# Weight blocks that are not written back, stores on a second queue, and regrouped visits, in a two-layer hybrid encoder

## The chip, the cores and the metric

The kernel runs on one core of a Trainium2 chip. Its time is the device time in microseconds of one execution; lower is better.

## The reference

Two layers of a mixer are applied to a prompt of 1024 rows and to 8 × 16 sample rows, with a model width of 1024. In each layer a projection `w_in` feeds three mixers whose outputs are gated, concatenated, projected by `w_out` and added to the input under a layer norm:

```python
h = x @ w_in
uA, vA, zA, qB, fB, iB, zB, qC, kC, vC, zC = jnp.split(h, split_pts, axis=-1)
yA, vA_rows = sgu(uA, vA, ln_v_g, ln_v_b, w_s, b_s)            # A: spatial gating
oB, S_new = hgrn2_scan(qh, kh, vh, logf)                       # B: linear recurrence
oC = swa_prompt(q, k, v, sinks)                                # C: windowed attention
mix = jnp.concatenate([yA, yB, yC], axis=-1)
out = layer_norm(DEEPNORM_ALPHA * x + mix @ w_out, ln_g, ln_b)
```

The recurrence B keeps a 64 × 64 state for each of 4 heads and goes chunk by chunk. The attention C has 8 query heads and 2 key heads, chunks of 64 and a window of 128, so that a tile of 128 rows sees at most two bands of keys, its own tile and the one before.

## The kernel before

Rows are cut into tiles of 128; eight tiles of the prompt and one of samples (`"s"`) form three groups of three tiles (`GROUPS`, L45). The kernel goes through the groups of layer 0, then those of layer 1, six in all. Within a group the columns of the projection are cut into blocks of 256. The order of blocks and side work in a group is a string (L47): for the first one `K Q0 Q1 -BX +C +X I F Q +B ZB U Z -C C0 C1 +N -X V +A`. A name is a weight block, + starts a piece of side work, - finishes it. K, Q0, Q1 are columns of the attention (blocks 9, 7, 8 of `w_in`), I and F those of the recurrence (5 and 4); after them come blocks 3, 6, 0, 2, 10, 11, 1 of `w_in`. Later groups also run the four `w_out` blocks O0 to O3 of the group before.

A product is made in three passes from high and low parts of both operands, so each weight block (1024 × 256 numbers, 1 MB) is split on chip. `issue_w` (L270 to L315) takes the next block of the list `wlist`. Where the block is met for the first time, it is loaded raw from DRAM in four pieces of 256 KB (L297) into the staging ring `wst` (four buffers; the first three blocks borrow others); `piece` (L299 to L312) then makes the high part `wh` with a copy on ACT (L125) and the low part `wl` with a subtraction on DVE or POOL (L142), and after each second piece stores 512 KB of either part to DRAM (L306, L307), on SP's queue. Where a layer's later groups meet the block again, both parts are loaded back (L288, L289), 2 MB. `wh` and `wl` have two buffers each.

A block's matmuls are written in `prod` (L349 to L359): 24 matmuls of 128 rows of depth each, eight with the high parts of both sides and two times eight with one low part. `tok_major` makes a result of 128 × 256 for a tile, `feat_major` one of 128 × 384 for 128 columns and all tiles. After each such result `tick` runs one visit of every open lane of side work, and the lanes' small matmuls come between the 24 of one result and the 24 of the next. PE's order is thus written by hand; other engines and queues are ordered by the framework under priorities.

Lane C is the attention (`lane_c`, L501 on). Its work goes block by block (tile and key head) through stages that lie some visits apart: scores with masks (L459, L466), softmax on DVE and ACT (L470 to L480), transposes of the probabilities (`p_transpose`, L488, copied by ACT to one of three `pT` buffers), and `attend` (L497), the product with the values. A block has two visits for each stage; of its two bands one is treated in each:

```python
                if ph == 0:
                    pso[u] = AXT([P, 2, P])
                if ph < len(bs):
                    attend(g, pso[u], bs[ph][1], pps.pop((u, ph)), ph == 0, ph == len(bs) - 1,
```

Lane B is the recurrence (`lane_b`, L669 on), a few visits for each tile. In a tile's first visit PE transposes keys (L682, copied by ACT to `kvt`), makes decay sums (L688, copied by ACT to `w4s`, a `t1b` buffer), and the chunk-local scores `psA` (L701 to L716), which DVE masks. Then `fin` runs for the tile before (L732): it transposes that tile's output, a `t1b` buffer that DVE has finished (L842), and splits the result into `mixh` and `mixl`. Then the transposes of `w4s` follow (L736). The next visit makes the new state's sums (`psk`, L771), the next the output (L826).

The sample tile and lanes A and X (spatial gating; transposes of x and output rows) are as they are in both kernels.

Of the kernel before, what the change touches and what calls it, by code (L numbers as in the profile page):

```python
# [8 lines left out]
F32 = mybir.dt.float32  # L9
# [11 lines left out]
P = 128  # L21
# [8 lines left out]
NC4 = 3  # L30
PPT = 1
NEA = 3
WDVE0 = (0, 1, 2, 3)
ACT_NORM = (3, 2, 4, 4, 1, 0)
POOL_OPS = ('mgzfy', 'mDrVyf', 'mgDrzVXQfw', 'mgzf', 'mgDrVyf', 'mgrVQfw')
# [61 lines left out]
def body(ctx: ExitStack, tc: tile.TileContext, A, O, cst):  # L97
# [22 lines left out]
    def AXT(shape):  # L120
        uid[0] += 1
        return ps_ax.tile(shape, F32, tag="ax", name=f"ax_{uid[0]}")
# [152 lines left out]
    def issue_w(off=WP):  # L275
        if wpos[0] >= len(wlist):
            return
        l, name, blk = wlist[wpos[0]]
        early = wpos[0] if wpos[0] < NEA else None
        eng_lo = WDVE0 if early is not None else WDVE[l]  # L280
        wpos[0] += 1
        key = (l, name, blk)
        with tc.high_priority(offset=off):
            wh, wl = T("wh", [P, 8, CB], 2, F32R), T("wl", [P, 8, CB], 2, F32R)
            if key in kept:
                for h in range(2):
                    ks = slice(4 * h, 4 * h + 4)
                    nc.sync.dma_start(wh[:, ks, :].bitcast(F32), kept[key][0][:, ks, :])  # L288
                    nc.sync.dma_start(wl[:, ks, :].bitcast(F32), kept[key][1][:, ks, :])  # L289
                wq.append((wh, wl))  # L290
                return
            nm = f"{name}{l}_{blk}"
            kept[key] = [dp.tile([P, 8, CB], F32, tag=nm + c, name=nm + c) for c in "hl"]
            for kk in range(4):
                tag, bufs = ("wst", NWST) if early is None or kk == 3 else ("pT", 3) if early % 2 == 0 else ("c4", NC4)
                st = T(tag, [P, 2, CB], bufs)
                ld = nc.sync.dma_start(st, A[name][l, :, blk, 2 * kk:2 * kk + 2, :])  # L297

                def piece(kk=kk, st=st, tag=tag, bufs=bufs, ld=ld):  # L299
                    hw, lw = wh[:, 2 * kk:2 * kk + 2, :], wl[:, 2 * kk:2 * kk + 2, :]  # L300
                    with tc.high_priority(offset=WP):
                        copy(hw, st)
                        up = tt(dve if kk in eng_lo else pool, lw, st, hw.bitcast(F32), ALU.subtract)
                        if kk % 2:
                            ks = slice(2 * kk - 2, 2 * kk + 2)
                            nc.sync.dma_start(kept[key][0][:, ks, :], wh[:, ks, :].bitcast(F32))  # L306
                            nc.sync.dma_start(kept[key][1][:, ks, :], wl[:, ks, :].bitcast(F32))  # L307
                    acquire(tag, bufs, ld)
                    release(tag, up)
                pieces.append(piece)  # L310
        wq.append((wh, wl))
# [190 lines left out]
    def lane_c(l, tiles, qks, vvs, vprev, oT, vd):  # L502
        todo = [(tl, t) for tl, t in enumerate(tiles) if t != "s"]
        nt = len(todo)
        smp = nt < 3
        blocks = []
        for n, (tl, t) in enumerate(todo):
            for g in range(2):
                bs = [(1 - t % 2, vvs[tl - 1] if tl else vprev)] if t else []
                blocks.append((n, tl, t, g, bs + [(t % 2, vvs[tl])]))  # L510
        qT = transposes(qks[0], todo[0][1] % 2)
        yield
        pts, pps, pso = {}, {}, {}
        nb = len(blocks)
        for k in range(2 * nb + LATT):
            u, ph = divmod(k - LATT, 2)
            if 0 <= u < nb:
                n, tl, t, g, bs = blocks[u]
                if ph == 0:
                    pso[u] = AXT([P, 2, P])  # L520
                if ph < len(bs):
                    attend(g, pso[u], bs[ph][1], pps.pop((u, ph)), ph == 0, ph == len(bs) - 1,
                           oT[:, :, tl * P:(tl + 1) * P])
            u, ph = divmod(k - LPT, 2)
            if 0 <= u < nb:
                bs = blocks[u][4]
                if ph < len(bs):
                    pps[(u, ph)] = p_transpose(pts[u], bs[ph][0], ph == len(bs) - 1)
            u, ph = divmod(k, 2)
            if ph == 0 and u < nb:  # L530
                n, tl, t, g, bs = blocks[u]
                pts[u] = scores(l, t, g, qT)
                if g == 1 and n + 1 < nt:
                    qT = transposes(qks[todo[n + 1][0]], todo[n + 1][1] % 2)
            yield
        if smp:
            yield from attn_sample(l, qks[2], vd, oT[:, :, 2 * P:3 * P])
# [131 lines left out]
    def lane_b(l, tiles, q2, kk, G, zb, vts):  # L669
# [5 lines left out]
        for tl, t in enumerate(tiles):  # L675
# [50 lines left out]
            for u in range(2):  # L726
                au = AT.rearrange("p (c u) t -> p u c t", u=2)[:, u]
                tt(dve, au, psA[u][:, :, 0:64], mA.unsqueeze(1).to_broadcast([P, 2, 64]), ALU.mult)
                for w in range(2):
                    ws = slice(32 * w, 32 * w + 32)  # L730
                    dve.copy_predicated(au[:, :, ws], m4[:, ws].unsqueeze(1).to_broadcast([P, 2, 32]), psA[u][:, :, 64:96])
            if fin is not None:  # L732
                fin()
            psw = AXT([P, 2, P])
            for i in range(2):
                pe.transpose(psw[:, i, :], w4s[:, i, :], idn)  # L736
# [26 lines left out]
                put_state(0)  # L763
            yield

            if not smp:
                psk = [AXT([P, 2, 64]) for _ in range(2)]
                for c in range(2):
# [393 lines left out]
```

## Time and profile before

| | |
|---|---|
| time, median of three runs | 1124.96 us (1124.52 to 1125.7) |
| the profiled execution's own time | 1125.85 us |
| its span | 1124.1 us |
| PE busy | 1080.9 us (96%) |
| DVE, ACT, POOL busy | 652.5, 503.8, 367.8 us |
| mean granted TensorE clock | 0.979 |
| DMA: one hardware queue | 272.66 MB, 69.1% of 16 engines' span |

The span is what lies between the first and the last instruction of the profiled execution; its own time is 1.75 us more. In a row of a timeline the first number is the start in us, the second how long a run of like instructions lasted; the brackets tell how long the engine was idle before and what ended that. Matmuls follow one another in the pipeline, so a row's end overlaps the next row's start; distances between starts tell what a group costs. "PEclk" is the clock that TensorE was granted, as a share of the full one.

### The profile page before, as it was taken

The numbers are of one execution on the slowest core, as the hardware profiler recorded it, in microseconds if no ns is written. First come the engines' busy times: TensorE is split into PE (matmuls) and PEld (weight loads), VectorE is DVE, ScalarE is ACT, GpSimd is POOL, SyncE is SP. The second block draws the span as 40 slices with busy tenths as digits, with TensorE's granted clock in tenths as the row PEclk, the third lists the DMA queues.
The fourth block names the chain that finished last, engine by engine and source line by source line (L and its number), as shares of the span: only waits on it lengthen the run. The fifth ranks groups of instructions, "written<-read, shape, count | busy, mean of one in ns | idle before, by whom it ended". The sixth has DMA issues, their size and how long they took to land. (4 is left out here: it accounts for less than half of the span.)

```text
span 1124.1 us, 25834 instructions
## 1 busy us (share of the span) xinstructions
PE 1080.9 (96%) x10267; PEld 1003.2 (89%) x10267; DVE 652.5 (58%) x1704; ACT 503.8 (45%) x1277; POOL 367.8 (33%) x490
## 2 busy tenths in 40 slices
PE   8598899999999999999999998999999999999996
PEld 7597789989899998998999897999989999889996
DVE  3359753765285355366459668457545636736744
ACT  5286743554433276334256754346443323443310
POOL 3135434432044102384304456141315121214502
PEclk9698999999999999999999999999999999999998
DMA  9994568867557647656966998776856685476463
GB/s 327 362 328 161 197 232 300 298 240 278 199 201 269 235 164 260 234 207 228 343 225 221 324 330 289 244 269 247 275 183 233 208 274 187 173 280 226 155 224 131
DMA packets 88521, 274.31 MB, mean 244 GB/s; under 512 B 10448, under 2 KB 14032, under 8 KB 88400
## 3 DMA queue, kind: packets, MB, share of 16 engines
q1 hardware_dynamic: 88400, 272.66, 69.1%
q8 instruction: 81, 1.33, 0.5%
q14 instruction: 40, 0.33, 0.1%
HBM read 193.97 MB, written 78.64 MB: 243 GB/s over the span
## 5 line engine op out<-in xcount | busy, mean ns | idle before, releaser
L142 POOL TENSOR_TENSOR wl<-wst,wh 128x512 fp32r<-128x512 f32 x58 | 84.6, 1472 | 210.2 <-ACT wh L125 126.2
L359 PE MATMUL mm<-wh,xh 128*128 128x256 f32 x864 | 129.7, 292 | 16.2 <-ACT wh L125 16.0
L359 PEld LDWEIGHTS mm<-wh,xh 128*128 128x128 f32 x864 | 113.1, 194 | 22.2 <-ACT wh L125 17.4
L384 POOL TENSOR_TENSOR sm<-sm,ct 128x4 f32<-128x4 f32 (+2 forms) x42 | 49.5, 1179 | 233.9 <-DVE sm L383 226.3
L359 PE MATMUL mm<-wh,xl 128*128 128x256 f32 x864 | 124.4, 287 | 0.0
L359 PE MATMUL mm<-wl,xh 128*128 128x256 f32 x864 | 122.7, 285 | 0.0
L359 PE MATMUL mm<-xh,wh 128*128 128x384 f32 x576 | 121.4, 353 | 0.0
L359 PEld LDWEIGHTS mm<-wh,xl 128*128 128x128 f32 x864 | 114.2, 196 | 0.1
L359 PE MATMUL mm<-xh,wl 128*128 128x384 f32 x576 | 112.0, 335 | 1.2 <-POOL wl L142 1.2
L359 PEld LDWEIGHTS mm<-wl,xh 128*128 128x128 f32 x864 | 113.1, 194 | 0.0
L359 PE MATMUL mm<-xl,wh 128*128 128x384 f32 x576 | 112.4, 336 | 0.0
L359 PEld LDWEIGHTS mm<-xh,wh 128*128 128x128 f32 x576 | 99.5, 192 | 5.9 <-issue 2.9
L359 PEld LDWEIGHTS mm<-xh,wl 128*128 128x128 f32 x576 | 100.8, 188 | 1.6 <-POOL wl L142 1.6
L359 PEld LDWEIGHTS mm<-xl,wh 128*128 128x128 f32 x576 | 102.0, 190 | 0.0
L142 DVE TENSOR_TENSOR wl<-wst,wh 128x512 fp32r<-128x512 f32 x61 | 61.5, 1015 | 67.1 <-ACT wh L125 52.7
L359 PE MATMUL mm<-wh,mixh 128*128 128x256 f32 x576 | 84.9, 290 | 1.5 <-ACT mixh L125 1.5
L125 ACT ACTIVATE wh<-wst 128x512 fp32r<-128x512 f32 x119 | 69.5, 625 | 34.3 <-DMA wst<-in_w_in 19.0
L359 PE MATMUL mm<-wh,mixl 128*128 128x256 f32 x576 | 80.8, 283 | 0.0
L359 PE MATMUL mm<-wl,mixh 128*128 128x256 f32 x576 | 80.8, 283 | 0.0
L473 ACT ACTIVATE c<-ax,sm 128x256 f32<-128x256 f32 (+1 forms) x128 | 57.3, 461 | 47.9 <-DVE sm L470 38.5
L359 PEld LDWEIGHTS mm<-wh,mixh 128*128 128x128 f32 x576 | 73.7, 191 | 1.7 <-ACT mixh L125 1.7
L359 PEld LDWEIGHTS mm<-wl,mixh 128*128 128x128 f32 x576 | 74.3, 192 | 0.0
(212 smaller groups left out, 1875.2 us busy)
## 6 DMA issues: line engine op xcount, KB each, us to landing
wst<-in_w_in SPq DMA_DIRECT2D x87, 256.0 KB, 5.5
xrow<-x SPq DMA_DIRECT2D x18, 512.0 KB, 4.5
wst<-in_w_out SPq DMA_DIRECT2D x32, 256.0 KB, 5.3
x<-xrow SPq DMA_DIRECT2D x9, 512.0 KB, 6.7
xrow<-in_xT SPq DMA_DIRECT2D x8, 512.0 KB, 5.8
wh<-w_in_9h SPq DMA_DIRECT2D x8, 512.0 KB, 5.1
wl<-w_in_9l SPq DMA_DIRECT2D x8, 512.0 KB, 7.6
xrow<-in_x_prompt SPq DMA_DIRECT2D x8, 512.0 KB, 4.9
```

Of the source, the lines that this page charges most:

```text
L125: return act.activation(o, i, AF.Copy)
L142: return e.tensor_tensor(o, a, b, op=op)
L359: pe.matmul(out, a(k), b(k), start=n == 0, stop=n == 23)
L384: pool.tensor_tensor(out, out, mh[:, :out.shape[-1]], op=ALU.pow)
L473: acquire("c4", NC4, *[act.activation(pt[:, h, sl], pss[h // 2][:, h % 2, sl], AF.Exp, bias=nM[:, h:h + 1], scale=0.125, accum_out=rs[:, h ...
```

## The change

Four things change.

1. `NFIRST = 5`: the first five blocks of the list (K, Q0, Q1, I, F of the first group) are split as before but not stored, and not remembered as kept. The second group therefore meets them as new: it loads them raw, splits them and stores both parts, and the third group loads the parts back. All other blocks are as before.
2. Where high parts are stored, ACT issues the store instead of SP (64 stores). Low parts stay on SP.
3. `attend` of both bands is done in a block's second visit, one behind the other. 28 of the 60 move by a visit; blocks with one band have the same matmuls, their output buffer being taken later.
4. `fin` is called at the start of the recurrence's second visit, ahead of `psk`, instead of within the first. Twelve of its 18 calls move; the last of each group stands where it was.

```diff
+NFIRST = 5
...
-        early = wpos[0] if wpos[0] < NEA else None
+        first = wpos[0]
+        early = first if first < NEA else None
...
-            nm = f"{name}{l}_{blk}"
-            kept[key] = [dp.tile([P, 8, CB], F32, tag=nm + c, name=nm + c) for c in "hl"]
+            keep = None
+            if first >= NFIRST:
+                nm = f"{name}{l}_{blk}"
+                keep = kept[key] = [dp.tile([P, 8, CB], F32, tag=nm + c, name=nm + c) for c in "hl"]
...
-                        if kk % 2:
+                        if kk % 2 and keep:
                             ks = slice(2 * kk - 2, 2 * kk + 2)
-                            nc.sync.dma_start(kept[key][0][:, ks, :], wh[:, ks, :].bitcast(F32))
-                            nc.sync.dma_start(kept[key][1][:, ks, :], wl[:, ks, :].bitcast(F32))
+                            nc.scalar.dma_start(keep[0][:, ks, :], wh[:, ks, :].bitcast(F32))
+                            nc.sync.dma_start(keep[1][:, ks, :], wl[:, ks, :].bitcast(F32))
...
-                if ph == 0:
-                    pso[u] = AXT([P, 2, P])
-                if ph < len(bs):
-                    attend(g, pso[u], bs[ph][1], pps.pop((u, ph)), ph == 0, ph == len(bs) - 1,
-                           oT[:, :, tl * P:(tl + 1) * P])
+                if ph == 1:
+                    pso = AXT([P, 2, P])
+                    for b in range(len(bs)):
+                        attend(g, pso, bs[b][1], pps.pop((u, b)), b == 0, b == len(bs) - 1, oT[:, :, tl * P:(tl + 1) * P])
...
-            if fin is not None:
-                fin()
             psw = AXT([P, 2, P])
...
             yield
 
+            if fin is not None:
+                fin()
             if not smp:
                 psk = [AXT([P, 2, 64]) for _ in range(2)]
```

What moves on the engines stands at three places. The first is SP's list where the fourth piece of block I is loaded (`wst` behind `lnb` and the stores of Q1, `w_in_8h` and `w_in_8l`; lines of the changed kernel have numbers one to four higher). Before:

```order
L208 DMA xrow_2048<-in_xT 128x1024
L224 DMA lng_2496<-in_ln_g 128x1024
L224 DMA lnb_2498<-in_ln_b 128x1024
L306 DMA w_in_8h<-wh_280 128x1024
L307 DMA w_in_8l<-wl_281 128x1024
L306 DMA w_in_8h<-wh_280 128x1024
L307 DMA w_in_8l<-wl_281 128x1024
L297 DMA wst_392<-in_w_in 128x512
L306 DMA w_in_5h<-wh_382 128x1024
```

Now:

```order
L301 DMA wst_370<-in_w_in 128x512
L209 DMA xrow_2016<-in_xT 128x1024
L209 DMA xrow_2018<-in_xT 128x1024
L225 DMA lng_2520<-in_ln_g 128x1024
L225 DMA lnb_2522<-in_ln_b 128x1024
L301 DMA wst_372<-in_w_in 128x512
L301 DMA wst_489<-in_w_in 128x512
```

The stores before and between the loads are gone, and the piece's load stands right behind the two constants; the loads of the next block, F, follow it.

The second is ACT's list ahead of the first tile's kvt copy in the first group. Before, with names of the staging buffers `wst`, the scores' exponentials `c` and the attention's `pT`:

```order
L656 ACTIVATE X_1037<-X_1037 128x1024
L480 ACTIVATE c_112_884<-c_112_884,sm_867 128x256 x3
L377 ACTIVATE tanh_982<-mm_957 128x256
L125 ACTIVATE wh_945<-wst_955 128x512
L125 ACTIVATE kT<-ax_1017 64x128
L125 ACTIVATE qT_1027<-ax_1028 64x512
L125 ACTIVATE oT_498<-ax_1107 128x2x128
L125 ACTIVATE pT_1116<-ax_1111 128x512
L377 ACTIVATE tanh_1099<-mm_1074 128x256
L125 ACTIVATE kvt_1121<-ax_1118 128x256
```

Now, where L310 is the store of a high part:

```order
L310 DMA w_in_0h<-wh_911 128x1024
L126 ACTIVATE pT_903<-ax_898 128x512
L126 ACTIVATE wh_911<-wst_921 128x512
L659 ACTIVATE X_1007<-X_1007 128x1024
L484 ACTIVATE c_112_854<-c_112_854,sm_837 128x256 x3
L126 ACTIVATE oT_476<-ax_954 128x2x128
L381 ACTIVATE tanh_948<-mm_923 128x256
L310 DMA w_in_0h<-wh_911 128x1024
L126 ACTIVATE kT<-ax_987 64x128
L126 ACTIVATE qT_997<-ax_998 64x512
L126 ACTIVATE pT_1082<-ax_1077 128x512
L126 ACTIVATE kvt_1087<-ax_1084 128x256
```

Two stores of block 0 stand in ACT's list behind the copies that they store; with those of blocks 3 and 6 higher up there are six ahead of the kvt copy.

The third is PE's list in the third group of layer 0, between O blocks, where `ax` is a PSUM buffer of side work, `vv` the values and `mm` a weight block's result. Before:

```order
L427 MATMUL ax_5356<-idn,qk_4608 128x128 x4
L359 MATMUL mm_5365<-wh_5057,mixh 128x256 x8
L359 MATMUL mm_5365<-wh_5057,mixl 128x256 x8
L359 MATMUL mm_5365<-wl_5058,mixh 128x256 x8
L497 MATMUL ax_5392<-pT_5277,vv_2180 64x256 x2
L488 MATMUL ax_5395<-idn,c_642_5224 128x128 x4
L359 MATMUL mm_5408<-wh_5236,mixh 128x256 x8
L359 MATMUL mm_5408<-wh_5236,mixl 128x256 x8
L359 MATMUL mm_5408<-wl_5237,mixh 128x256 x8
L497 MATMUL ax_5392<-pT_5314,vv_4609 64x256 x2
L488 MATMUL ax_5445<-idn,c_642_5224 128x128 x4
```

Now:

```order
L431 MATMUL ax_5416<-idn,qk_4668 128x128 x4
L363 MATMUL mm_5425<-wh_5117,mixh 128x256 x8
L363 MATMUL mm_5425<-wh_5117,mixl 128x256 x8
L363 MATMUL mm_5425<-wl_5118,mixh 128x256 x8
L492 MATMUL ax_5452<-idn,c_662_5284 128x128 x4
L363 MATMUL mm_5465<-wh_5296,mixh 128x256 x8
L363 MATMUL mm_5465<-wh_5296,mixl 128x256 x8
L363 MATMUL mm_5465<-wl_5297,mixh 128x256 x8
L501 MATMUL ax_5499<-pT_5334,vv_2164 64x256 x2
L501 MATMUL ax_5499<-pT_5374,vv_4669 64x256 x2
L492 MATMUL ax_5505<-idn,c_662_5284 128x128 x4
```

The first band's attend has gone from ahead of the first transposes to just ahead of the second band's attend.

## Rows read from the trace of the kernel before

**Rows 1.** The page's first part: busy us, share of the span and instructions of PE

```profile
PE 1080.9 (96%) x10267; PEld 1003.2 (89%) x10267; DVE 652.5 (58%) x1704; ACT 503.8 (45%) x1277; POOL 367.8 (33%) x490
```

**Rows 2.** Waits of PE: engine, line, operation, waited for; total us, times, longest

```profile
PE mm L359 <- ACT wh L125: 16.0, 4, 13.1
...
PE ax L497 <- ACT pT L125: 2.6, 1, 2.6
PE ax L701 <- ACT kvt L125: 2.5, 1, 2.5
...
PE mm L359 <- POOL wl L142: 1.2, 1, 1.2
```

**Rows 3.** Timeline of PE around 36 to 49: start us, us, instructions, idle before

```profile
35.15 0.88 PE L359 MATMUL mm<-wh,xh 128*128 128x256 f32 x6
49.18 0.80 PE L359 MATMUL mm<-wh,xh 128*128 128x256 f32 x2 [13.15 <-ACT wh L125]
```

**Rows 4.** Timeline of SP, the issuing queue, around 35 to 38

```profile
34.76 0.38 SPq L306 DMA_DIRECT2D w_in_8h<-wh  x1
...
38.27 0.33 SPq L297 DMA_DIRECT2D wst<-in_w_in  x1
```

**Rows 5.** The load issued at 38.27: issue to landing

```profile
DMA to landing us min/median/max: 10.2/10.2/10.2
```

**Rows 6.** Windows: stretch and its us; busy us of each engine; granted clock; DMA

```profile
36.00:49.20 13.20, 0.05 (x2) 0.03 (x1) 1.81 (x7) 0.63 (x1) 0.08 (x1) 0.58 1.03 391
49.20:56.60 7.40, 7.40 (x39) 7.40 (x40) 2.59 (x5) 4.33 (x9) 1.77 (x2) 0.59 1.03 387
56.60:92.00 35.40, 35.34 (x250) 33.44 (x248) 23.19 (x58) 31.40 (x82) 14.75 (x19) 1.00 0.90 301
532.00:560.00 28.00, 28.00 (x244) 27.39 (x244) 13.91 (x29) 9.72 (x22) 10.48 (x7) 1.00 0.94 348
672.00:698.00 26.00, 21.56 (x334) 18.99 (x332) 23.80 (x58) 13.22 (x30) 17.66 (x20) 0.98 0.88 307
698.00:712.00 14.00, 13.79 (x105) 13.27 (x106) 7.28 (x25) 5.31 (x13) 3.03 (x3) 0.79 0.65 215
```

**Rows 7.** Timeline of PE around 653

```profile
653.78 0.51 PE L359 MATMUL mm<-wh,xh 128*128 128x256 f32 x2 [0.82 <-ACT wh L125]
```

**Rows 8.** Instructions of the high-part store's line on SP: ns min/median/max

```profile
L306 SPq DMA_DIRECT2D w_in_3h<-wh x4: 320/384/495, 64.3 to 613.8; - x4
...
L306 SPq DMA_DIRECT2D w_out_0h<-wh x4: 319/521/1033, 191.8 to 739.1; - x4
```

**Rows 9.** Timeline of PE, attention visits between weight blocks, 763 to 775

```profile
763.46 1.12 PE L359 MATMUL mm<-wl,mixh 128*128 128x256 f32 x8
...
765.81 1.12 PE L359 MATMUL mm<-wh,mixl 128*128 128x256 f32 x8
...
771.28 1.12 PE L359 MATMUL mm<-wl,mixh 128*128 128x256 f32 x8
772.33 0.65 PE L497 MATMUL ax<-pT,vv 128*64 128x256 f32 x4
772.91 0.66 PE L488 MATMUL ax<-idn,c 128*128 128x128 f32 x4
...
774.36 1.12 PE L359 MATMUL mm<-wh,mixl 128*128 128x256 f32 x8
```

**Rows 10.** Timeline of PE, the two output transposes that wait

```profile
677.56 0.44 PE L842 MATMUL ax<-idn,t1b 128*128 128x128 f32 x2 [1.17 <-DVE t1b L142]
...
698.21 0.69 PE L842 MATMUL ax<-idn,t1b 128*128 128x128 f32 x2 [3.02 <-DVE t1b L142]
```

**Rows 11.** Timeline of ACT, the copies that the second transposes read

```profile
675.27 0.38 ACT L125 ACTIVATE t1b<-ax 128x256 f32<-128x256 f32 x1
...
696.38 0.39 ACT L125 ACTIVATE t1b<-ax 128x256 f32<-128x256 f32 x1
```

**Rows 12.** Waits of SP, the queue's own

```profile
SPq L306 <- ACT wh L125: 130.9, 30, 13.9
```

More of the change, by code (lines that the diff above doesn't have):

```diff
@@ L512, in lane_c @@
         yield
-        pts, pps, pso = {}, {}, {}
+        pts, pps = {}, {}
         nb = len(blocks)
```

## The prediction

> **What bounds the kernel now.** I read the page first: PE is busy for 1080.9 of the 1124.1 us of the span [rows 1]. So TensorE is the bound, and whatever does not take work from PE, close one of its gaps or raise its clock is worth nothing. Second, the waits of PE [rows 2]: one wait stands out, 16.0 us on the weight copies of ACT, of which one alone is 13.1; two of about 2.5 are on the recurrence's and the attention's copies, and one of 1.2 on a low part from POOL. Third, the timeline of PE around the long one [rows 3]: the sixth matmul of a group of eight ends at 36.0, the other two start at 49.18. I has four pieces, a quarter of the block's depth each, and these two are the first that need the fourth.
>
> What that piece waited for shows on the queue. SP issued its load at 38.27, the fifth issue since 34.76 [rows 4]; it landed 10.2 us later, at 48.47 [rows 5], and 0.7 us after that, ACT having copied it, PE went on. From 36 to 49.2 the DMA engines were full: share 1.03, 391 GB/s, while ACT did 0.63 us of work [rows 6]. In the single queue, and so ahead of the piece, stand twelve stores: of K, Q0 and Q1 two halves each of the high and the low part, 524 KB apiece, 6.3 MB. After the stall PE ran at a granted clock of 0.59 until 56.6 [rows 6], about the lower of its two levels: the idle time before it is followed by slow work.
>
> **The change, part by part, against the profiled execution's 1125.85 us.**
>
> *Five blocks unstored.* Twelve stores less ahead of the piece are 6.3 MB / 391 GB/s = 16.1 us of full transfer engines. The order of SP shows the load right behind lng and lnb. It would land at about 48.5 − 16.1 = 32.4 and be copied 0.7 us later, before PE runs dry at 36.0. Three microseconds are left over, so I take the whole 13.1 us as gained. What is late next is no weight: F's loads follow directly, 1 MB for some 8 us of matmuls. The clock comes back with it: 7.4 us at 0.59 instead of 1 are 7.4 × 0.41 = 3.0 us. Term: −16.1. Bound below: −8, if the later pieces and constants queue up behind and half is lost again.
>
> *Second group of layer 0.* There the same five blocks are now loaded raw (1 MB) instead of as parts (2 MB), split, and stored: 20 more copies on ACT, ten subtractions each on DVE and POOL, 10 MB of stores, 5 MB less of loads. The trace has this very work elsewhere: layer 1's first blocks at 532 to 560, transfer share 0.94, PE 28.00 of 28 busy, ACT 9.72, DVE 13.91, POOL 10.48 [rows 6]. So it is hidden: cost 0. If the cover goes, the price is that of the same work later in layer 1, where PE waited 1.2 us for a low part [rows 2] and 0.8 for a copy [rows 7]: up to +2.0.
>
> *High-part stores on ACT.* 64 issues leave SP and enter ACT's instruction stream. On SP one takes about 0.38 us, at worst 1.03 [rows 8]. ACT is no bound over the span, so only stretches count where PE waits for it. The first is 56.6 to 92, ACT busy 31.40 of 35.40 [rows 6], after which PE waits 2.5 us for the kvt copy [rows 2]; the order puts six stores (blocks 3, 6, 0 of w_in) ahead of that copy. The second is the end of the attention of the first group, where PE waits 2.6 us for pT [rows 2], with one store ahead. 7 × 0.38 = +2.7. Ends: 0, if they fall into ACT's own waits; 7 × 1.03 = +7.2. I take the middle price because SP's loaded median is nearest to an issue under a full queue. What the issue waits for on ACT no row shows; that is the fourth rival.
> On the transfers the move alone gives nothing in this sum, since what filled the engines was bytes. The Trainium skill, page "DMA: Bandwidth & Descriptors", section "Issuing engines are not separate DMA queues", says so too: transfers started from different engines end on the same 16 DMA engines, and only issuing time is saved. By it alone this part is a pure cost, +2.7 rather than a gain, as I have put it; it would speak against this part of the change.
>
> *Attention visits.* In a visit with the transposes alone, PE goes from 763.46 to 765.81: 2.35 us with sixteen matmuls of a weight block. With an attend as well it takes 771.28 to 774.36, 3.08 us [rows 9]. An attend by itself costs 0.73. From its first to the next group's start it takes 772.33 to 772.91, 0.58; directly behind another attend no more than this is paid, so at least 0.15 is saved, and at most 0.30 if those 0.58 hold the same start-up once more. I take 0.2 for each block with two bands. There are 14 in each layer; the four of layer 0's first group wait on ACT anyway, so 24 × 0.2 = −4.8 (bounds 24 × 0.15 = −3.6 and 28 × 0.30 = −8.4). The attend that is moved is held back by nothing new: its pT was copied a visit before.
>
> *Output transposes.* Two of the 18 now make PE wait: 1.17 us at 677.56 and 3.02 at 698.21, both for t1b from DVE [rows 10]. Moved a visit later they come behind 24 matmuls. At 677.56 the next thing PE needs, the w4s copy, was started at 675.27 on ACT [rows 11], done long before: 1.17 gained. At 698.21 that copy started at 696.38 and took 0.39 [rows 11], so PE, dry at about 695.2, still waits until 696.8 or so: 1.6 us remain and 1.4 are gained. After the 3.02 the clock was 0.79 over the 14 us from 698 to 712 [rows 6]: 14 × 0.21 = 2.9 us lost. PE also stood still for 1.17 us at 677.56, and the clock of 672 to 698 is 0.98 [rows 6], so that gap cost hardly any; 1.6 lies nearer to that than to 3.02, so I count the clock as kept. Term: −(1.17 + 1.4 + 2.9) = −5.5. Bounds: 0 (DVE, busy 23.80 of 26 in 672 to 698 [rows 6], is as late for psk's operands as it was for t1b) and −7.1.
>
> **Sum.** −16.1 + 0 + 2.7 − 4.8 − 5.5 = −23.7, so 1125.85 − 23.7 = 1102.2. The median of the three runs, 1124.96, lies 0.9 below the profiled execution: 1101.3, put at **1101**.
>
> **Rivals.**
> 1. *Given back in the first group.* What is early meets ACT and DVE at work: ACT is nearly full in 56.6 to 92, and if weights come 13 us earlier while ACT's list before the kvt copy is the same, PE waits there. For: 31.40 of 35.40 busy, six issues more. Against: in the stall ACT did 0.63 us of work in 13.2 [rows 6], so it loses no lead. Only −8 of the −16.1 would stay and the issues cost +7: 1101 + 8 + 4 = 1113.
> 2. *Loads overtake the stores.* If the stores on ACT's queue share the transfer engines with the loads instead of standing ahead of them, the late pieces of layer 1 come in time: the 1.2 at 636 and the 0.8 at 653.78 [rows 2, 7] go too, 1101 − 2 = 1099. For: in [rows 5] a load took 10.2 us behind stores. Against: half the bytes, the low parts, stay on SP. The Trainium skill, same page, section "Queues, rings and completion order", states that a DMA engine takes packets in turn from the queue rows that have work; by this rule the rival would hold, and no run here shows it yet.
> 3. *The change doesn't do what it says to the stall.* The fourth piece may be held not by stores but by its buffer, whose last reader is a subtraction of an earlier piece. For: SP made five issues in 3.8 us [rows 4], slower than it can, so something held it. Against: issued at 38.27 it still took 10.2 us, and those follow the bytes. If the buffer decides, the issue comes no sooner than 38.27; 262 KB at 391 GB/s are 0.7 us and the copy is 0.7, so PE goes on at 39.7 at best: 3.7 us of the stall stay and the clock falls all the same, 1101 + 3.7 + 3.0 = 1108.
> 4. *Slower: ACT held by its own stores.* The completion semaphores are dealt out in turn over all issues, so an issue on ACT waits, where SP used to, for an earlier transfer, and everything behind it on ACT (copies, exponentials, evictions) waits too. Some 30 stores lie in stretches whose transfer share is about 0.9 or more. It decides from a mean of 23.7 / 30 = 0.8 us that PE sees for each; at 1.2 us it would be 1101 + 36 = 1137. For: the five issues of [rows 4]. Against: SP's own account has its h-stores wait for ACT's copies, 130.9 us over 30 of them [rows 12], not for transfers, and ACT, issuing right behind its own copy, has that wait behind it.
>
> **Chances.** Forecast 0.60; given back 0.16; overtaking 0.10; stall kept in part 0.05; slower 0.06; no change, by some mixture that cancels, 0.03. Two measurements of this kernel differ by about 0.2% (2.2 us); all but the last two cases lie below that: faster 0.91, same 0.03, slower 0.06. The range: the forecast with its bounds (attention up to −8.4, issues 0 or the transposes at nothing) and the overtaking reach from 1101 − 2.7 − 3.6 − 2 = 1093 up to 1101 + 5.5 + 4.5 = 1111, and the given-back case at 1113 is to be in: 1093 to 1114.
>
> **What would show it.** Right: no gap of PE over 1 us between 30 and 57 and a clock at 1 there; the page's wait of L359 on ACT's wh near 3 instead of 16.0; the wait of the output transposes on t1b gone; the span near 1100. In the first group, ACT rows of stores near 0.4 us. Wrong: ACT stores that take or idle over 1 us each in the stretches of 0.9 (rival 4); a stall of 5 us or so at I's fourth piece with its load issued at about 38 (rival 3); a kvt wait of much over 5 us near 85 (rival 1); and new waits of PE on wh or wl at the second group's start, which I price at nothing.

## The result, and the profile after

The changed kernel takes 1106.42 us (median of four runs, 1104.96 to 1107.71) against 1124.74 for the kernel before, run beside it: a ratio of 0.984, 95% interval 0.9817 to 0.9863, so 18 us less with an uncertainty of some 2.6. Forecast were 1101 and 1093 to 1114. The time lies in the range, 5 above the forecast; the terms behind it fared worse than their sum.

The page of the changed kernel, the lines that answer to [rows 1] and those of the DMA queues (packets, MB, share of 16 engines' span):

```profile
PE 1069.6 (97%) x10267; PEld 1003.1 (91%) x10267; DVE 664.2 (60%) x1714; ACT 513.2 (46%) x1297; POOL 379.1 (34%) x500
...
q1 hardware_dynamic: 79184, 233.86, 61.1%
q10 hardware_dynamic: 9216, 33.56, 7.9%
```

PE has 11 us less busy time (the mean granted clock is 0.989 instead of 0.979, and attends cost less) and some 7 us less idle time. There is now a second hardware queue, q10, with the 33.56 MB of the high parts. The waits of PE, where [rows 2] had 16.0 us on the weight copies:

```profile
PE ax L829 <- ACT vt L126: 4.2, 2, 2.9
PE mm L363 <- DVE t3k L383: 3.3, 3, 1.7
PE ax L774 <- DVE AQ L739: 2.9, 1, 2.9
PE ax L774 <- DVE kT L143: 2.3, 1, 2.3
PE ax L588 <- DVE c L143: 2.1, 1, 2.1
...
PE mm L363 <- ACT wh L126: 1.9, 3, 1.0
```

The wait on `wh` has fallen from 16.0 to 1.9. In its place stands a list of waits of 1 to 3 us on side work, most of them new: the state's copies `vt`, the factors `AQ` and `t3k`, the sample attention's `c`. The largest four make up 12.7 us.

At the place of [rows 3], PE's timeline no longer has a gap; SP's has the fourth piece as the first of five loads issued from 22.88 on, where it had been issued at 38.27 [rows 4]; ACT copied it at 32.99, right behind an eviction:

```profile
35.39 1.12 PE L363 MATMUL mm<-wh,xh 128*128 128x256 f32 x8
36.35 1.12 PE L363 MATMUL mm<-wh,xl 128*128 128x256 f32 x8
```

```profile
22.88 11.84 SPq L301 DMA_DIRECT2D wst<-in_w_in  x5
```

```profile
32.99 0.62 ACT L126 ACTIVATE wh<-wst 128x512 fp32r<-128x512 f32 x1
```

The windows of the changed kernel (columns as in [rows 6]) show the clock at its upper level behind that place, and what is new in the second group:

```profile
44.00:56.00 12.00, 12.00 (x84) 12.00 (x83) 7.53 (x18) 9.82 (x34) 2.73 (x2) 1.00 0.65 209
250.00:262.00 12.00, 12.00 (x104) 11.15 (x103) 10.97 (x24) 6.32 (x13) 8.53 (x14) 1.00 0.63 231
262.00:287.00 25.00, 22.92 (x222) 20.36 (x221) 8.15 (x34) 11.65 (x53) 0.59 (x1) 0.93 0.57 192
```

**Where the time went, stage by stage.** PE makes 252 products of 24 matmuls in the same order in all kernels, so the start of the same product in two timelines tells how far one kernel is ahead. Products 30, 72, 114, 156 and the last, 251, start at 174.04, 356.11, 533.79, 718.19 and 1111.38 us before, and at 157.99, 344.38, 520.14, 702.48 and 1092.97 now. The first two mark the end of the first and of the second group's own blocks; differences of neighbours give the stages. The lower rows are from the experiments below. Each number is a difference to the kernel before, of one profiled execution each; a single clock dip that one execution has and another has not moves such a number by 1.5 us, as is shown below.

| kernel | to product 30 | to 72 | to 114 | to 156 | to 251 | all |
|---|---|---|---|---|---|---|
| change | −16.1 | +4.3 | −1.9 | −2.1 | −2.7 | −18.4 |
| blocks unstored alone | −16.9 | +2.5 | +0.1 | −0.1 | 0.0 | −14.3 |
| stores on ACT alone | +2.8 | 0.0 | 0.0 | −1.0 | 0.0 | +1.8 |
| attention visits alone | −2.1 | −1.3 | −1.9 | −1.8 | −2.4 | −9.5 |
| output transposes alone | −1.8 | +0.1 | −0.1 | −2.0 | 0.0 | −3.8 |
| sum of the four | −18.0 | +1.3 | −1.9 | −4.9 | −2.3 | −25.8 |
| change without stores on ACT | −19.1 | +3.2 | −2.0 | −5.9 | −3.2 | −27.0 |
| change without output transposes | −15.7 | +2.1 | −1.9 | +0.3 | −3.2 | −18.4 |

The sum of the four single parts is −25.8, near the forecast's −23.7; done together they give −18.4. The loss is 1.9 in the first group, 3.0 in the second and 2.8 in layer 1's first group. Most of it goes with the stores on ACT: without them the other three add up as a whole (−14.3 − 9.5 − 3.8 = −27.6 against −27.0). Stage by stage they do not: the sums of the three are −20.7, +1.3, −1.9, −3.9 and −2.4, so 1.6 and 1.9 are still missing in the first two groups, and 2.8 more come in layer 1.

### The profile page after: what moved, and what is told of

Its sections match the earlier page's. It is cut to its first block, busy times and chain, and to the rows that moved or that the text cites. A ratio compares the mean times of both kernels' runs of the same rounds, so it can differ in the third digit from the quotient of the medians.

```text
span 1105.6 us, 25914 instructions
## 1 busy us (share of the span) xinstructions
PE 1069.6 (97%) x10267; PEld 1003.1 (91%) x10267; DVE 664.2 (60%) x1714; ACT 513.2 (46%) x1297; POOL 379.1 (34%) x500
## 3 DMA queue, kind: packets, MB, share of 16 engines
q10 hardware_dynamic: 9216, 33.56, 7.9%
## 5 line engine op out<-in xcount | busy, mean ns | idle before, releaser
L143 POOL TENSOR_TENSOR wl<-wst,wh 128x512 fp32r<-128x512 f32 x68 | 97.8, 1449 | 200.2 <-ACT wh L126 129.4
L126 ACT ACTIVATE wh<-wst 128x512 fp32r<-128x512 f32 x139 | 81.8, 625 | 44.2 <-DMA wst<-in_w_in 21.7
L143 DVE TENSOR_TENSOR wl<-wst,wh 128x512 fp32r<-128x512 f32 x71 | 70.9, 1007 | 51.1 <-ACT wh L126 46.2
```

The costliest lines, as they stand in the source:

```text
L126: return act.activation(o, i, AF.Copy)
L143: return e.tensor_tensor(o, a, b, op=op)
```

## The experiments

Ratios are to the kernel before, run beside each of them.

### One part at a time

The first part alone (e1_first; `nc.sync` kept for both stores):

```diff
-                        if kk % 2:
+                        if kk % 2 and keep:
...
                             nc.sync.dma_start(keep[0][:, ks, :], wh[:, ks, :].bitcast(F32))
```

> The kernel before with the first part alone: the first five blocks are not stored, all other stores stay on SP, attention visits and output transposes as before. Forecast's account: -16.1 us from the stall and 0 in the second group, about 1109. Account from the two traces, matmul by matmul: -15.5 up to the I block, then some +5 in the second group of layer 0 (steps of +0.7, +0.9 and +3.7 with DVE and POOL as releasers), about 1114 to 1115. Rival: the second group's loss belongs to the stores on ACT or to the regrouped attention, and this kernel comes out at 1109 with no gap of PE over 1 us between 150 and 300.

Measured: 1112.71, ratio 0.9887 (0.9871 to 0.9903), 13 us less. The stall is gone: product 12 starts 15.8 us earlier, 15.5 of it won between products 9 and 12, that is across the stall. In the second group 2.5 come back, most of it here, on PE's timeline:

```profile
266.01 0.41 PE L589 MATMUL ax<-idn,c 128*128 128x128 f32 x2 [1.77 <-DVE c L143]
```

PE waits for `c`, the sample attention's softmax on DVE. There was no such wait before. So part of the second group's loss belongs to the first part by itself; the change loses more there (+4.3, although the attention gives 1.3; 1.5 of it is a lower clock behind the wait, which this kernel doesn't have).

The second part alone (e2_act):

```diff
-                            nc.sync.dma_start(kept[key][0][:, ks, :], wh[:, ks, :].bitcast(F32))
+                            nc.scalar.dma_start(kept[key][0][:, ks, :], wh[:, ks, :].bitcast(F32))
```

> The kernel before with the second part alone: high parts are stored from ACT's queue, all blocks stored. Forecast's account: 64 issues on ACT cost 2.7 us, transfers gain nothing: 1127, stall at I unchanged at 13. Rival (loads overtake the stores): the loads on SP stand behind half the bytes only, the stall at I shrinks from 13.1 to some 5 to 9 us and the two waits of 1.2 and 0.8 in layer 1 go: 1115 to 1121.

Measured: 1128.67, ratio 1.0021 (1.0004 to 1.0038), 2.4 us more. The stall did shrink, but not for the reason of the rival. ACT's timeline (the idle time of a held store stands with the instruction behind it):

```profile
19.22 0.33 ACTq L306 DMA_DIRECT2D w_in_7h<-wh  x1
19.59 0.63 ACT L125 ACTIVATE wh<-c 128x512 fp32r<-128x512 f32 x1 [5.16 <-DMA pT<-in_w_in]
...
24.50 0.33 ACTq L306 DMA_DIRECT2D w_in_7h<-wh  x1
24.88 0.28 ACT L125 ACTIVATE vv<-mm 128x128 f32<-128x128 f32 x1 [3.97 <-DMA wst<-in_w_in]
...
32.81 0.33 ACTq L306 DMA_DIRECT2D w_in_8h<-wh  x1
33.18 0.63 ACT L125 ACTIVATE wh<-pT 128x512 fp32r<-128x512 f32 x1 [6.72 <-DMA bs<-in_bs]
```

Between 14 and 33 us ACT stood idle for 5.2, 4.0 and 6.7 us, each time ahead of a store of Q0 or Q1, with copies and evictions queued behind the store. By the brackets each idle stretch ended with the landing of an earlier load. On PE's timeline these became waits on evictions (`vv`, `qk`), and with the slower groups behind two of them the stall at I starts 9.2 us later (the six matmuls ahead of it start at 44.34 instead of 35.15):

```profile
20.44 1.22 PE L359 MATMUL mm<-wh,xh 128*128 128x256 f32 x8 [2.28 <-ACT vv L125]
...
34.13 1.21 PE L359 MATMUL mm<-wh,xh 128*128 128x256 f32 x8 [2.89 <-ACT qk L125]
...
49.84 0.80 PE L359 MATMUL mm<-wh,xh 128*128 128x256 f32 x2 [4.61 <-ACT wh L125]
```

It ends at 49.84, though; before it was 49.18. The fourth piece landed no sooner: its load was issued at 36.94, 1.3 us earlier than before, and by the view of that load

```profile
DMA to landing us min/median/max: 12.2/12.2/12.2
```

against 10.2 in [rows 5]. So this load did not overtake the stores. What passed was a store: the second high half of Q1, issued on ACT at 34.63, landed after 7.9 us, ahead of a low half that SP had issued at 33.15 (11.2 us). The two waits of layer 1 that the overtaking was to remove are still there, 1.10 us on `wl` at 639 and 0.80 on `wh` at 656. The fourth rival's mechanism, ACT held by its own stores, is real: ACT's idle time just ahead of its 64 stores sums to 16.0 us, nearly all of it at four stores. Here the stall hid it.

The third part alone (e3_attend; the diff of the change's lines in `lane_c`):

```diff
-                if ph < len(bs):
-                    attend(g, pso[u], bs[ph][1], pps.pop((u, ph)), ph == 0, ph == len(bs) - 1,
...
+                    for b in range(len(bs)):
+                        attend(g, pso, bs[b][1], pps.pop((u, b)), b == 0, b == len(bs) - 1, oT[:, :, tl * P:(tl + 1) * P])
```

> The kernel before with the third part alone: both bands' attends in one visit. Forecast's account: 0.2 us for each of 24 blocks, -4.8, about 1120. Account from the two traces: a visit that loses an attend is 0.73 shorter and one that has two is 0.43 longer, 0.30 a block, 28 blocks: -8.4 at most, 1116 to 1118.

Measured: 1115.37, ratio 0.9903 (0.9881 to 0.9926): 11 us less by the runs, 9.5 by the two timelines. In the steady visits the account of 0.73 less and 0.43 more holds, as PE's timeline of the changed kernel shows where [rows 9] were:

```profile
748.25 1.12 PE L363 MATMUL mm<-wl,mixh 128*128 128x256 f32 x8
...
750.60 1.12 PE L363 MATMUL mm<-wh,mixl 128*128 128x256 f32 x8
...
760.44 1.08 PE L501 MATMUL ax<-pT,vv 128*64 128x256 f32 x8
761.45 0.66 PE L492 MATMUL ax<-idn,c 128*128 128x128 f32 x4
```

A visit with transposes alone is still 2.35 (748.25 to 750.60). Two attends in a row take 760.44 to 761.45, 1.01 us, where one took 0.58: the second costs 0.43, not 0.58, and a block saves 0.30. The 28 blocks make 8.4 by that; the rest of the 9.5 is the balance of waits that came out shorter (1.41 instead of 2.56 on `pT` at 140 us, none on `wl` at 636) and others that came out longer. (The attends of the four blocks with one band move by a visit as well, so 32 of the 60 move; for these four nothing is saved.)

The fourth part alone (e4_fin):

```diff
-            if fin is not None:
-                fin()
             psw = AXT([P, 2, P])
...
+            if fin is not None:
+                fin()
             if not smp:
```

> The kernel before with the fourth part alone: output transposes one visit later. Forecast's account: -5.5, about 1119. Account from the two traces: the waits of 1.17 and 3.02 on t1b go, and waits of the output matmuls on the state's copies (vt) of about the same length come in the next visits: 0 to -1.5, 1123 to 1125.

Measured: 1122.46, ratio 0.9982 (0.9968 to 0.9995), 2 us less; 3.8 by the timelines. Both waits on t1b are gone, and on PE's timeline a wait of 2.44 on `vt`, the state's copy, stands in the next visit:

```profile
687.76 1.23 PE L826 MATMUL ax<-vt,AQ 128*64 128x64 f32 x14 [2.44 <-ACT vt L125]
688.92 2.81 PE L359 MATMUL mm<-xh,wh 128*128 128x384 f32 x8
```

In this execution the clock stayed lower only for the first group of eight behind it (2.66 to the next start, then the usual 1.39).

### One part undone

u_fin, the transposes back in the first visit (the last diff reversed in the changed kernel):

> The changed kernel with the fourth part undone: output transposes back in the first visit. Account of the sum: the part gives here what it gave alone (-3.3), so 1106 + 3 = 1109 to 1110. Account of the traces: in the changed kernel the transposes' waits of 1.2 and 3.0 were traded for waits of 1.2 and 2.9 of the output matmuls on vt, with the clock falling after the longer one as before; undoing it brings the t1b waits back and takes the vt waits away: 1105 to 1107.

Measured: 1107.74, ratio 0.9833 (0.9814 to 0.9852): the same as with them. By the timelines the whole is level too (+0.0), but by amounts of both signs. At the place of the two waits undoing the part costs 2.7 us (products 146 to 153, 644 to 691 us): 1.1 is back on t1b at 661 and 2.5 at 683, and the long `vt` wait is only 1.2 shorter. That is the same as in the fourth part alone, which won 2.8 between the same products. Before that place the kernel without the part is 2.2 ahead, won at 167 us, at 268 to 274 and at 615, 1.5 of it because the clock did not fall behind the wait on `c`. That the part has anything to do with these is not shown. So the account of the traces had the time right, and half of the reason: the `vt` waits answer for a part of the old waits, not for all.

u_act, high parts stored from SP:

```diff
-                            nc.scalar.dma_start(keep[0][:, ks, :], wh[:, ks, :].bitcast(F32))
+                            nc.sync.dma_start(keep[0][:, ks, :], wh[:, ks, :].bitcast(F32))
```

> The changed kernel with the second part undone: high parts stored from SP again. Account of cost: as alone, the stores on ACT cost 2 to 3 us, most of it in the first group, so 1103 to 1104, with the new waits between 67 and 95 us shorter. Rival (overtaking loads): the waits of 1.2 and 0.8 on wl and wh at 622 and 639 come back and no wait in the first group shrinks: 1107 to 1109.

Measured: 1099.91, ratio 0.9764 (0.9749 to 0.978), which doesn't touch the change's interval: 8.6 us by the ratios, 8.6 by the timelines (3.0 in the first group, 1.2 in the second, 3.8 in layer 1's first, 0.5 later). The price of a store, ACT's timeline in layer 1, with stores on ACT:

```profile
634.46 0.63 ACT L126 ACTIVATE wh<-wst 128x512 fp32r<-128x512 f32 x1 [2.94 <-DMA wst<-in_w_in]
635.12 0.33 ACTq L310 DMA_DIRECT2D w_in_6h<-wh  x1
635.49 0.63 ACT L126 ACTIVATE wh<-wst 128x512 fp32r<-128x512 f32 x1 [0.40 <-DMA wst<-in_w_in]
```

and without, two copies in a row:

```profile
628.38 1.31 ACT L126 ACTIVATE wh<-wst 128x512 fp32r<-128x512 f32 x2 [1.89 <-DMA wst<-in_w_in]
```

The second copy starts 1.03 us after the first instead of some 0.68, so a store takes about 0.35 us of ACT, 64 of them 22 us. That is the forecast's 0.38. Holds by earlier transfers are nearly gone in the changed kernel: over its 64 stores ACT's idle time just ahead of a store sums to 1.2 us, since the first stores now come at 47 us, after the crowd. What was too small was the number of places. Without the stores on ACT 3.0 us come back at one place of the first group, where a wait of 2.3 us of L774 on `kT` from DVE at 94.44 is gone, 0.8 at 191 us, and 3.8 in layer 1's first group, in steps between 613 and 669 us, where of the waits on `vt` that of 1.24 is gone and that of 2.92 is down to 2.21. `vt` is copied by ACT; why the wait on `kT` hung on ACT's stores stays open, and no single store is traced to a wait.

u_first, all blocks stored again:

```diff
-NFIRST = 5
+NFIRST = 0
```

> The changed kernel with the first part undone (all blocks stored in the first group, high parts from ACT). If the parts add up: 1125.7 + 2.9 - 10.4 - 3.3 = 1115, with a stall of about 5 at I and evictions held behind stores at 20 and 34 us as in the second part alone. If the first part cost more in company (the second group's loss of some 4 and new waits from 67 to 95), then it gives only some 5 here: 1111.

Measured: 1114.16, ratio 0.9889 (0.9874 to 0.9903). Beside the change the first part gives 5.5 us by the ratios (7.4 by the timelines), where alone it gave 13. By the timelines it gives 14.6 in the first group, where without it the holds and a stall of 4.5 at 49.68 are back, and costs 5.7 in the second (8.99 − 14.64), 1.6 later. The sum (1115) was met.

### The state's order on DVE

```diff
+            eo = dve.tensor_copy(EG, ...)
+            tc.add_manual_dep(eo.ins, after_s.ins.name, ...)
```

This is s_first3; the same order is given to the products that make X.

> The changed kernel with one order fixed by hand: on DVE the next tile's decay factors (X, egl, EG) stand behind the present tile's state update. Account: in the changed kernel the state at 674.4 stood behind idle time and seven products of the next tile, and PE waited 2.9 for its copy; now the copy comes 1 to 1.5 us earlier, the wait falls to 1.4 to 2 and, if the clock stays up, 2 us more come back: 1102 to 1104. Rival: the products that now come later make the next tile's first matmuls late by as much, and the time stays at 1106.

Measured: 1107.66, ratio 0.9828 (0.9813 to 0.9843): no gain. PE's timeline has the wait on `vt` down as expected, from 2.92 to 1.95, and a new one before it:

```profile
618.30 2.55 PE L363 MATMUL mm<-xh,wh 128*128 128x384 f32 x8 [2.23 <-DVE t3k L383]
...
675.67 0.89 PE L835 MATMUL ax<-vt,AQ 128*64 128x64 f32 x14 [1.95 <-ACT vt L126]
```

At 618 PE waits 2.23 for `t3k` on DVE (0.70 in the change). That wait is not shown to come from the order: PE reached the place 1.3 us sooner than in the change and was released at nearly the same time (618.04 there), and DVE was not full (5.99 of the 12 us from 606 to 618); it had waited for ACT, and ACT 3.09 us for the load of a weight piece. With a slower group behind the wait 3.1 us are lost here. The rival shows one visit behind the `vt` wait, where the copy of `w4s` is waited for, 1.38 us at 685.88 (none there in the change). So 1.3 us were won at 676, 0.7 of it was lost right behind, and the loss at 618 stays unexplained.

### The second group's loss

These four start from u_act. The first, g1_other:

```diff
+            if first >= NFIRST and l == 0 and name == "w_in":
+                key = (l, name, {9: 3, 7: 6, 8: 0, 5: 2, 4: 10}.get(blk, blk))
             if key in kept:
```

> The kernel u_act (the change with high parts stored from SP) in which layer 0's later groups take, for the five blocks that were not stored, the kept parts of five other blocks; so their loading raw, splitting and storing in the second group is left out (the output is then that of other weights). Account: the second group's loss of about 3 us that the first part showed alone is this work, on DVE and POOL; the waits of 1 to 2 us on qT and c between 150 and 265 shrink and the kernel takes 1099.9 - 3 to - 4 = 1096. Rival: the loss comes from the order of the side work, and the time stays within 1 us of u_act.

Measured: 1095.86, ratio 0.9739 (0.9719 to 0.9758). This kernel leaves out the second split of all five blocks, so its output is that of other weights. By the timelines, against u_act, 3.83 us come back between products 56 and 58, at 263 us: the wait on `c` is gone. The other steps of the second group stay below 0.5, so the rest of the added work there is hidden, as forecast.

The second, p_lo:

```diff
+        if NFIRST <= first and l == 0 and name == "w_in" and blk in (4, 5):
+            eng_lo = ()
```

> The kernel u_act with the low parts of the blocks I and F in the second group all subtracted on POOL instead of half on DVE. Account: at 252 to 255 two subtractions on DVE take 3.3 us just ahead of the sample attention's chain on DVE, for whose last product (c) PE then waits 2.1 us, after which the clock falls; without them the wait goes and some 3 us come back, 1097. Rival: DVE is late for other reasons (decay factors of the sample tile), the wait stays near 2 and the time at 1100.

Measured: 1100.56, ratio 0.9778 (0.9756 to 0.9801): no gain, the wait at 263.61 is 2.7 instead of 2.1. DVE's timeline without the change of engine:

```profile
252.10 3.26 DVE L143 TENSOR_TENSOR wl<-wst,wh 128x512 fp32r<-128x512 f32 x2
...
256.29 2.19 DVE L143 TENSOR_TENSOR X<-X,t3k 128x128 f32<-128x128 f32 x4
```

with it:

```profile
253.68 0.55 DVE L385 SCALAR_TENSOR_TENSOR t3k<-tanh,mm 128x384 f32<-128x384 f32 x1 [1.56 <-ACT tanh L383]
...
254.68 3.49 DVE L143 TENSOR_TENSOR X<-X,t3k 128x128 f32<-128x128 f32 x4
```

and with the split left out (g1_other):

```profile
250.98 0.90 DVE L143 TENSOR_TENSOR X<-X,t3k 128x128 f32<-128x128 f32 x4 [0.84 <-ACT X L661]
...
252.37 1.90 DVE L143 TENSOR_TENSOR X<-X,t3k 128x128 f32<-128x128 f32 x4
```

Free of the two subtractions, DVE waited 1.56 us for ACT's `tanh`, and its four products of X took 3.49 us instead of 2.19, or 1.90 without any split. Four products of the same shape just before, with POOL idle for most of the time, took 0.90 in all three kernels; beside those of 1.90 and 2.19 POOL had four small products (`W`), beside those of 3.49 the subtractions first. With the change of engine ACT's timeline has I's four copies ahead of that `tanh`, and POOL's has the four subtractions beside the products:

```profile
251.09 2.18 ACT L126 ACTIVATE wh<-wst 128x512 fp32r<-128x512 f32 x4
253.18 0.47 ACT L383 ACTIVATE tanh<-mm 128x384 f32<-128x384 f32 x1
```

```profile
251.84 5.21 POOL L143 TENSOR_TENSOR wl<-wst,wh 128x512 fp32r<-128x512 f32 x4 [1.74 <-ACT wh L126]
```

So the loss is not one engine's: the same block's copies, and its subtractions on either engine, stand in the way of a chain that goes through ACT and DVE. The account "two subtractions on DVE" fell.

The third, n3_sp:

```diff
-NFIRST = 5
+NFIRST = 3
```

> The kernel u_act with only the first three blocks (K, Q0, Q1) unstored, so I and F are stored in the first group. No store then stands ahead of I's fourth piece, so by the account of the forecast the stall stays away; F's and I's eight stores queue ahead of the loads of the next blocks instead, where PE has work, and the second group has two blocks less to split at 246 to 265: 1097. Rival: those stores make the loads of blocks 3 and 6 late, a new wait on wh of a few us appears between 45 and 70: 1102 or more.

Measured: 1099.56, ratio 0.9768 (0.9753 to 0.9784): level with u_act, by two opposite amounts. The second group wins its 3.8 back; the first loses 3.8 by product 30, with longer waits on `t3k` (2.41 instead of 1.67) and on `pT` (2.42 instead of 1.58) and a new one of 1.48 on the state, though no wait on `wh` behind the first blocks. Both accounts held by half.

The fourth, i_kept:

```diff
-            if first >= NFIRST:
+            if first >= NFIRST or first == 3:
```

> The kernel u_act with four blocks unstored (K, Q0, Q1, F): only I, which the second group splits at 246 to 255 just ahead of the sample attention, is stored in the first group. Account: the split that g1_other took away costs 3.8 us at one place, where I's copies and subtractions stand ahead of that chain, so that place gives 3.8 us back, and the first group, with four stores instead of eight between 36 and 60, loses less than the 3.9 of n3_sp: 1096 to 1098. Rival: the first group's loss in n3_sp comes with I's stores, and the time stays at 1099 to 1100.

Measured: 1098.03, ratio 0.9746 (0.973 to 0.9762), the lowest median of all but g1_other, though its interval overlaps u_act's. Its profiled execution, the slowest of its four runs, shows the same 3.8 won at 264 us, so that it is block I whose split costs this; 2.8 are lost by product 30, and 2.7 more by product 156, where PE waits 2.04 at 677 instead of 0.45. The version to keep is one of these two; both beat the change by their intervals.

## Why the prediction was right in sum and wrong in several terms

**The stall: right.** Forecast −16.1 for stall and clock, measured −15.5 across the stall, in the first part alone and in the change. The landing was put at 32.4; ACT copied the piece at 32.99. With the load issued at 22.88 the third rival, by which the buffer would hold it until 38.27, is out.

**"So it is hidden: cost 0", second group: wrong.** Measured +2.5 alone, and 3.83 for the one place at 263 us in g1_other and in i_kept. The step took layer 1's raw blocks at 532 to 560 as the precedent [rows 6]. That stretch carries the bytes but not the side work: at 250 to 267 the sample attention's softmax goes through ACT and DVE, and there DVE is busy for 10.97 of 12 us. The bound (+2.0) came from a wait on weights; the wait that came was not on weights at all, and the lower clock after it (granted 0.52 from 268.2 to 271.7, about the lower of the two levels) cost nearly as much as the wait. PE's timeline in the changed kernel:

```profile
267.08 0.41 PE L588 MATMUL ax<-idn,c 128*128 128x128 f32 x2 [2.08 <-DVE c L143]
...
268.22 2.02 PE L363 MATMUL mm<-wh,xh 128*128 128x256 f32 x8
270.04 1.87 PE L363 MATMUL mm<-wh,xl 128*128 128x256 f32 x8
271.74 1.12 PE L363 MATMUL mm<-wl,xh 128*128 128x256 f32 x8
```

A wait of 2.08, then two groups of eight at 1.82 and 1.70 instead of 0.96, 1.6 us lost. The clock's part is not fixed by the wait. In u_fin the same wait was followed by a granted clock of 1.00 (268 to 271.7) and groups at the usual pace:

```profile
266.77 0.41 PE L588 MATMUL ax<-idn,c 128*128 128x128 f32 x2 [2.08 <-DVE c L143]
...
267.92 1.21 PE L363 MATMUL mm<-wh,xh 128*128 128x256 f32 x8
268.97 1.12 PE L363 MATMUL mm<-wh,xl 128*128 128x256 f32 x8
```

So the change's +4.3 is made of 2.2 for the wait, 1.5 for a clock dip that one execution had and another had not, and 1.6 at 167 and 195 us (the second a wait of 1.0 on `qT` from DVE), less 1.2 won by the attention.

**"7 × 0.38 = +2.7", stores on ACT: the price right, the number wrong.** The change loses 8.6 by them, against 1.8 in the second part alone. The step counted two places where PE waited for ACT before; it left out that the other parts, by taking PE's waits away, can make ACT the next to be waited for, as `vt` shows in layer 1's first group. The upper end (7 × 1.03 = +7.2) came near by accident.

**"0.2 for each block", attention: right mechanism, undersized.** 0.30 a block. The upper end (0.30) had been argued from the start-up of the first attend, and that is how it is: 0.58, then 0.43.

**"−5.5", output transposes: half of it.** By the ratios −2 alone and nothing in company (u_fin); at their place 2.8 by the timelines alone and 2.7 in company. The step looked for the next wait on the same engine's next instruction, the w4s copy, and found 1.6. The next wait stood one visit later: the state's copy `vt`, which PE now reached sooner and DVE no sooner. With 2.92 it was as long as the old one (in u_fin it is 1.75), and the clock fell behind it as before (PE, changed kernel):

```profile
675.24 1.24 PE L829 MATMUL ax<-vt,AQ 128*64 128x64 f32 x14 [2.92 <-ACT vt L126]
676.41 2.93 PE L363 MATMUL mm<-xh,wh 128*128 128x384 f32 x8
679.14 2.56 PE L363 MATMUL mm<-xl,wh 128*128 128x384 f32 x8
681.54 1.58 PE L363 MATMUL mm<-xh,wl 128*128 128x384 f32 x8
```

The measured time lies between the term and its bound at 0, and the reason given for the bound (DVE as late for the operands as it was for t1b) is what took the other half.

**The rivals.** Overtaking was refuted where it could be seen (12.2 us of landing against 10.2). The Trainium skill, page "DMA: Bandwidth & Descriptors", section "Queues, rings and completion order", has engines take packets from queue rows in turn; no row here shows a load that gained by it, but a store on ACT's queue did pass one on SP's (7.9 us against 11.2). The same page's section "Issuing engines are not separate DMA queues" says that transfers started from several engines share the same 16 DMA engines, which the 12.2 us agree with, and that the issuing time saved is small; here that time was not saved but moved to an engine that PE waits for, at 0.35 us each. "Given back" came true in the second group; in the first it shows only in the 3.0 that the stores on ACT took. "ACT held by its own stores" came true in the second part alone, 16 us, and is absent once the early stores are.

By the timelines, then, the forecast's terms against the measured ones: first part −16.1 and −14.3, attention −4.8 and −9.5, transposes −5.5 and −3.8, each of these three alone, and stores on ACT +2.7 and +8.6, in company. The errors, +1.8, −4.7, +1.7 and +5.9, sum to +4.7, and the rest of the 5.3 (−23.7 forecast, −18.4 measured) is what doesn't add. That the forecast came within 5 us is owed to errors of both signs.

## What to carry to other kernels

When a change removes one big wait, price its other edits against what is waited for after it: an issue, a subtraction or a copy that was free beside a stall is not free behind it. A precedent for "hidden work" must carry the same side chains, not just the same bytes. And a DMA issue belongs on a queue whose engine nobody waits for; here SP had the room and ACT did not.

## What the runs showed of the hardware that was not expected

- A store issued from ACT holds ACT's whole stream until it can be issued: 5.2, 4.0 and 6.7 us at 14 to 33 us in the second part alone, each until an earlier load had landed. In the changed kernel the price was about 0.35 us an issue.
- A load on SP's queue beside stores on ACT's took no less time to land (12.2 us) than behind all stores in one queue (10.2), while a store on ACT's queue (7.9 us) landed ahead of an earlier one on SP's (11.2).
- DVE is slowed by work on POOL: four products on DVE took 0.90 us with POOL idle for most of the time, 1.90 and 2.19 beside four small products on POOL, and 3.49 where POOL's four subtractions went on over the first two thirds. The Trainium skill, page "SBUF — State Buffer", section "Who interferes with whom", says that only the port pair shared by DVE and GpSimd contends, as an exclusive lock; the traces agree as far as DVE's time goes, and tell nothing of the lock itself.
- The clock fell after the waits of 2.08 and 2.92 us as it had after 13.15 and 3.02; after that of 1.77 in the first part alone it did not (1.05 for the next eight), nor after one of 2.08 at the same place in u_fin (1.05).
